# An encoder layer with its FFN in four blocks of 512 tokens, the later blocks' convolution and output projection placed inside the FFN

## The chip, the cores and the metric

The kernel runs on one core of a Trainium2 chip, as one program. Time is device microseconds. Three runs of the kernel before took 2814.54, 2819.62 and 2824.38 us, so its time is 2819.62 us (median). A further execution was taken by the hardware profiler; all rows below come from it.

The engines: PE is TensorE (matmuls and transposes), PEld its weight loads, DVE VectorE, ACT ScalarE, POOL GpSimd, SP the queue that issues every DMA of this kernel.

## The reference

One layer over 2048 prompt tokens of a new stream and 32 tokens of a running stream, all in float32:

```python
xn = rmsnorm(x, g_mix)
q, k, v, u, gate = split(xn @ w_in)                 # 1024 -> 2560
q, k = head_rmsnorm(q, g_q), head_rmsnorm(k, g_k)   # 8 heads of 64
z = q @ k.T * 64 ** -0.5                            # s < t only
sp = softplus(z)
a = exp(log_sigmoid(z) - (reverse_cumsum(sp) - sp)) # stick-breaking weights
o = a @ v
c = causal_dwconv(u * sigmoid(gate), w_dw, 31 taps) # 512 channels
c = silu(layernorm(c))
h = x + concat([o, c]) @ w_out                      # 1024 -> 1024
up = causal_dwconv(rmsnorm(h, g_ffn) @ w_up, 3 taps)# 1024 -> 5632
a, g = split(up)
y = h + (silu(g) * a) @ w_down                      # 2816 -> 1024
```

The running stream's 32 tokens see 1024 cached keys and values and carried convolution states; y, the new keys and values and the new states are returned.

## The kernel before

Every float32 product is three TensorE products. An operand is split into a high part in the rounded format F32R and a rest (`split`, L523: ACT copies the high part, DVE subtracts to get the rest); then high x high, high x rest and rest x high are added up in one PSUM bank. This holds for weights too: each w_in, w_out, w_up and w_down tile is loaded raw and split on chip.

Stages, in program order:

1. Input projection (L780 to L811). Granules of 256 columns of w_in, in two halves of 1024 tokens. u and gate become rows of `cb`, four SBUF tiles with one channel a partition and all tokens along the row (L636). q, k and v are normalised and go to DRAM.
2. Depthwise convolution (`conv`, L537), called once for each half of the tokens: for each of 4 channel tiles, 31 DVE instructions over 1024 or 1086 columns, each a multiply-add with one tap's weight from `wdw`.
3. Attention (`unit`, L861): for each head and each 256 queries, scores, sigmoid (ACT), a running product over the keys (a DVE scan in `survive`, L829), transposes on PE, a split, and the product with the values. The first units' tiles in SBUF take the place of the input projection's weights and tokens.
4. Output projection (`out_chunk`, L1021) in seven chunks of 256 tokens and a last one of 288. w_out is split once and stays in SBUF. The last chunk computes transposed, and the norm of the FFN's first segment is placed inside it (L1096).
5. FFN (L1166) in three segments of 768, 640 and 672 tokens (`SEGS`). For each of 22 column tiles f: `up` loads and splits two w_up tiles (512 KB each), makes 2 x 24 x 2 matmuls into two banks, applies the 3 taps on DVE, the gate, and loads and splits a w_down tile. After each second f, `down` adds two f's products to y. w_up and w_down are loaded and split in each of the three segments: 132 and 66 loads.

The order of instructions is not the program order. `Plan.run` (L231) is a list scheduler: it goes through the recorded steps with a price for each instruction and a latency between engines, and each engine takes the ready step of lowest rank, which is its place in the program. The convolution has ranks behind the whole attention (L1011), so DVE takes it only where nothing else is ready. Which SBUF place a tile takes is written out by hand (`SLOTS`, L46); a tile whose place is still being read has to wait. PSUM has 8 banks, and a rule in `run` keeps one of them for the oldest group that has none.

All DMAs are issued by SP in one order, each with its waits, so a DMA whose wait is late holds up those behind it.

## Time and profile before

| | |
|---|---|
| runs | 2814.54, 2819.62, 2824.38 us |
| profiled execution | 2816.1 us; span from first to last instruction 2814.2 us |
| busy share of the span | PE 96%, PEld 90%, DVE 71%, ACT 39%, POOL 18% |
| mean granted TensorE clock | 0.992 |
| HBM | 217.08 MB read, 64.11 MB written |
| DMA | mean 102 GB/s; 33.3% of the 16 engines' time |

A busy share says that an instruction was in the engine, and matmuls overlap, so a PE at 96% need not issue matmuls as fast as it could. The stages have different limits, so the page's mean is taken apart by stretches: input projection to 580 us, attention from 580 to 1098 us, output projection to 1307 us, FFN to 2810 us.

### The profile page before, as it was taken

The page shows a single profiled execution, that of the slowest core. Times are in us where ns is not written, and L with a number is a line of the kernel's source. Part 1 is how long each engine was busy: PE and PEld are TensorE (multiplying, and loading weights), DVE is VectorE, ACT ScalarE, POOL GpSimd, SP SyncE. Part 2 cuts the span into 40 slices and gives each one's busy share as a digit, 9 for nine tenths or more (in the row PEclk, how much of TensorE's full clock was granted, in tenths as well). Part 3 has the DMA queues.
Part 4 walks back from the last instruction along what each step waited for, and adds up shares of the span by engine and source line. Part 5 has one row for each costly group of instructions (what it writes and reads, how often), then busy time and mean ns, then how long its engine had stood idle before and what let it go on. Part 6 is the DMA issues. An engine that isn't in the chain of part 4 may idle for free.

```text
span 2814.2 us, 43546 instructions
## 1 busy us (share of the span) xinstructions
PE 2690.4 (96%) x17345; PEld 2527.0 (90%) x17345; DVE 2003.1 (71%) x2311; ACT 1103.1 (39%) x2179; POOL 494.3 (18%) x724
## 2 busy tenths in 40 slices
PE   8999999988888888999999999999999999999999
PEld 8999999977777877889999999999999999999998
DVE  6988888899989998345565656666666665656566
ACT  5267235566666675114222222322232233322222
POOL 1155035523223231011000000000000001101100
PEclk9999999999999999999999999999999999999999
DMA  4255224644333335555222222242222233222221
GB/s 161 64 177 175 76 82 152 192 130 116 85 93 85 93 99 159 182 159 170 68 60 68 60 63 72 89 159 71 75 83 75 73 99 103 80 73 64 83 61 70
DMA packets 299907, 288.29 MB, mean 102 GB/s; under 512 B 21591, under 2 KB 260077, under 8 KB 298679
## 3 DMA queue, kind: packets, MB, share of 16 engines
q1 hardware_dynamic: 299703, 285.50, 33.3%
q8 instruction: 136, 2.23, 0.3%
q14 instruction: 68, 0.56, 0.1%
HBM read 217.08 MB, written 64.11 MB: 100 GB/s over the span
## 4 chain that ended last, share of the span: by engine, by line
PE 73%; DVE 10%; issue 6%; POOL 6%; ACT 3%; DMA 2%; SPq 0%; POOLq 0%; DVEq 0%; ACTq 0%
PE bank L380 70%; DVE arena L409 6%; POOL few L409 3%; DVE arena_r L409 3%; PE bank L387 3%; POOL arena L409 3%; ACT arena L394 2%; ACT arena_r L394 1%; DMA arena<-in_cache_sb_v_dram 1%; SPq L434 0%; DMA arena<-arena 0%; DVE few L409 0%; DMA oT_d<-arena 0%; DMA arena<-in_w_ffn_dw_dram 0%; DMA qT_d<-arena_r 0%
## 5 line engine op out<-in xcount | busy, mean ns | idle before, releaser
L380 PE MATMUL bank<-arena_r 128*128 128x256 f32 (+8 forms) x15360 | 2494.5, 322 | 32.4 <-DVE arena_r L409 31.0
L380 PEld LDWEIGHTS bank<-arena_r 128*128 128x128 f32 x15360 | 2320.6, 190 | 157.1 <-DVE arena_r L409 43.3
L409 DVE TENSOR_TENSOR arena_r<-arena,arena_r 128x1024 fp32r<-128x1024 f32 (+5 forms) x398 | 421.7, 1068 | 466.2 <-ACT arena_r L394 462.8
L394 ACT ACTIVATE arena_r<-arena 128x1024 fp32r<-128x1024 f32 (+5 forms) x398 | 368.7, 935 | 911.1 <-PE bank L380 509.8
L394 ACT ACTIVATE arena<-bank 128x384 f32<-128x384 f32 (+15 forms) x770 | 327.6, 473 | 278.2 <-PE bank L380 244.4
L409 DVE TENSOR_TENSOR arena<-bank,arena 128x512 f32<-128x512 f32 (+2 forms) x458 | 281.8, 631 | 189.5 <-PE bank L380 189.2
L409 DVE TENSOR_TENSOR_SCAN arena<-arena 128x1024 f32<-128x1024 f32 (+11 forms) x200 | 330.4, 1680 | 15.1 <-ACT arena L394 7.8
L409 DVE SCALAR_TENSOR_TENSOR arena<-arena,wdw 128x1024 f32<-128x1024 f32 (+1 forms) x240 | 320.6, 1367 | 1.6
L387 PE MATMUL bank<-ident,arena 128*128 128x128 f32 (+4 forms) x1645 | 224.0, 279 | 67.2 <-DVE arena L409 50.6
L387 PEld LDWEIGHTS bank<-ident,arena 128*128 128x128 f32 (+4 forms) x1645 | 185.5, 142 | 100.0 <-DVE arena L409 57.0
L409 POOL COPY halo<-arena 128x2 f32<-128x2 f32 x176 | 80.4, 472 | 1061.8 <-ACT arena L394 1049.8
L394 ACT ACTIVATE arena_r<-bank 128x512 fp32r<-128x512 f32 (+4 forms) x422 | 218.2, 570 | 110.5 <-PE bank L387 98.2
L409 DVE SCALAR_TENSOR_TENSOR arena<-arena,wfd 128x768 f32<-128x768 f32 (+2 forms) x264 | 248.1, 940 | 10.2
L409 DVE TENSOR_TENSOR arena_r<-bank,arena_r 128x512 fp32r<-128x512 f32 (+2 forms) x334 | 194.2, 634 | 18.2 <-ACT arena_r L394 18.0
L409 POOL TENSOR_SCALAR_AFFINE_SELECT arena<-arena 128x128 f32<-128x128 f32 (+1 forms) x130 | 132.8, 1032 | 338.5 <-ACT arena L394 338.1
L394 ACT ACTIVATE arena<-arena 128x1024 bf16<-128x1024 f32 (+4 forms) x100 | 88.2, 882 | 254.3 <-DVE arena L409 237.1
L409 POOL TENSOR_SCALAR few<-few 128x1 f32<-128x1 f32 (+3 forms) x87 | 62.1, 713 | 493.1 <-DVE few L409 405.3
L409 POOL TENSOR_TENSOR few<-few,nhalf 128x1 f32<-128x1 f32 (+3 forms) x87 | 112.0, 1290 | 6.6
L409 DVE TENSOR_TENSOR arena<-arena 128x768 f32<-128x768 f32 (+4 forms) x78 | 68.7, 881 | 46.7 <-ACT arena L394 33.2
L394 ACT ACTIVATE arena<-bank,few 128x64 f32<-128x64 f32 (+1 forms) x272 | 68.6, 325 | 77.9 <-POOL few L409 77.9
L409 DVE TENSOR_SCALAR arena<-arena,wfd,bfd 128x768 f32<-128x768 f32 (+2 forms) x132 | 84.0, 637 | 6.0 <-ACT arena L394 6.0
L409 POOL COPY arena<-halo 128x2 f32<-128x2 f32 x132 | 24.5, 185 | 294.1 <-DVE arena L409 281.7
(43 smaller groups left out, 377.8 us busy)
## 6 DMA issues: line engine op xcount, KB each, us to landing
arena<-in_w_up_dram SPq DMA_DIRECT2D x132, 512.0 KB
arena<-in_w_down_dram SPq DMA_DIRECT2D x66, 512.0 KB
arena<-in_x_prompt_dram SPq DMA_DIRECT2D x32, 512.0 KB
arena_r<-qT_d SPq DMA_DIRECT2D x64, 256.0 KB
arena<-h_d SPq DMA_DIRECT2D x32, 512.0 KB
arena<-in_w_in_dram SPq DMA_DIRECT2D x24, 512.0 KB
arena<-in_w_in_dram SPq DMA_DIRECT2D x32, 256.0 KB
out_dram<-arena SPq DMA_DIRECT2D x32, 256.0 KB
```

Source lines behind the costliest of these rows:

```text
L380: lambda: nc.tensor.matmul(plan.real(out), lhsT, rhs, start=start, stop=stop),
L387: "pe", in_.shape[0] * (0.4167 if in_.dtype == F32R else 0.8333) + 2.5, lambda: nc.tensor.transpose(plan.real(out), in_, idt), [out], [in_ ...
L394: "act", ns, lambda: nc.scalar.activation(out, plan.real(in_), func, **kw), aps(out, kw.get("accum_out")), reads
L409: self.tag, self.price(name, n / (2 if fast else 1), pointers), lambda: fn(out, *map(plan.real, args), **kw), [out], aps(*args, *kw.values())
```

## The change

- The FFN runs in four blocks (`feed`) of 512 tokens, the last of 544 with the running stream's 32. A w_up tile then needs 24 matmuls of 512 columns into one bank, in the last block 48 of 272.
- Block 0 loads raw weights and splits them, in half tiles, and stores the split pairs in DRAM (`wu_d`, `wd_d`: 44 and 22 tiles of 1 MB). Blocks 1 to 3 load the pairs straight into the place that the matmuls read: 1 MB for each w_up and each w_down tile, through two places (`wu`) and three (`wd`).
- u x sigmoid(gate) goes to DRAM (`c_d`); `conv` works on blocks of 512 tokens and loads them from there. Blocks 0 and 1 are convolved behind the input projection as before, block 2 inside the FFN of block 1, block 3 inside that of block 2.
- The output projection (`project`) is cut into the part of the heads and that of the convolution, with h kept in DRAM between them, and into blocks: block 0 before the FFN, block b + 1 inside the FFN of block b. w_out is loaded raw and split for each use (`out_weights`), in the place `wu` that the FFN's weights use, eight pairs of tiles for a block and eight more for the running stream.
- `weave` and `tick` place these pieces: after each `up` part and each `down` tile half the side work is brought up to a given share.
- The planner's prices for matmuls and scans are new, and a new rule (`fits`) says when a group may take a bank ahead of older ones. Constants of the FFN are loaded at the start; several SBUF places are new.

```diff
-SEGS = ((0, 768, 0), (768, 640, 0), (1408, 640, 32))
+BLK = 512
+NBLK = T // BLK
 GRP = 2
...
+        def fits(k):
+            if place[k] == oldest:
+                return True
...
+            if place[k] - oldest > AHEAD:
+                return False
...
-            max(n * 0.4167, width(lhsT) * 0.8333) + 2.5,
+            max(n * 0.4167 + 13, 112),
...
-    vec = Engine("dve", nc.vector, lambda name, n, pointers: n / 0.96 + 68 + 61 * pointers)
+    def vec_price(name, n, pointers):
+        return n * 2.1 + 50 if name == "tensor_tensor_scan" else n / 0.96 + 68 + 61 * pointers
+    vec = Engine("dve", nc.vector, vec_price)
...
+    CB = 30 + T + 30 + TS
+    c_d = dram.tile([SB, CB], F32, name="c_d")[:]
+    wu_d = dram.tile([2 * FT, P, 2048], F32R, name="wu_d")[:]
+    wd_d = dram.tile([FT, P, 2048], F32R, name="wd_d")[:]
...
+    def conv(b):
...
+            pieces = [(b * BLK, BLK)] + ([(T + 30, TS)] if b == NBLK - 1 else [])
+            for t0, m in pieces:
+                src = slot("csrc", (544,))[:, : m + 30]
+                need = ["c0"] + [("c", x) for x in {max(b - 1, 0), b}]
+                dma(src, c_d[c * P : (c + 1) * P, t0 : t0 + m + 30], gets=need)
+                acc = slot("cacc", (m,))
+                for k in (30, *range(30)):
+                    w = wdw[:, k * CT + c : k * CT + c + 1]
+                    if k == 30:
+                        vec.tensor_scalar(acc, src[:, k : k + m], w, cvec[:, c : c + 1], ALU.mult, ALU.add)
+                    else:
+                        vec.scalar_tensor_tensor(acc, src[:, k : k + m], w, acc, ALU.mult, ALU.add)
+                    yield
+                o = t0 if t0 < T else T
+                dma(yT_d[c * P : (c + 1) * P, o : o + m], acc, puts=[("y", b if t0 < T else NBLK)])
...
+        key = [("c", grp[0] // 2)]
+        dma(c_d[ct * P : (ct + 1) * P, o : o + m], sig[:, :m], puts=key)
...
+    def out_weights(i):
+        nh, k = i // 4, i % 4 * 2
+        w = slot("wu", (2, 2, 512), F32R)
+        for j in range(2):
+            raw = slot("raw", (512,))
+            dma(raw, w_out[(k + j) * P : (k + j + 1) * P, nh * 512 : (nh + 1) * 512])
+            split(w[:, 0, j], w[:, 1, j], raw)
+        return w
...
+    def project(b, part, begin):
+        groups = [list(range(4 * b, 4 * b + 4))] + ([[16]] if b == NBLK - 1 else [])
+        for tl in groups:
+            w = sum(tokens(ti)[1] for ti in tl)
+            hi, lo = slot("cat", (CT, w), F32R), slot("cat", (CT, w), F32R)
+            for i in range(0, len(tl), 2):
+                some = tl[i : i + 2]
+                rs = slice(tokens(some[0])[0].start, tokens(some[-1])[0].stop)
+                cs = slice(i * P, i * P + rs.stop - rs.start)
+                fill = conv_out if part else heads_out
+                yield from fill(some, rs, rs.start // BLK, hi[:, :, cs], lo[:, :, cs])
+            for nh in range(2):
+                pss = [bank() for _ in tl]
+                for kk in range(2):
+                    wo = out_weights(4 * nh + 2 * part + kk)
+                    for i, ti in enumerate(tl):
+                        rows = tokens(ti)[1]
+                        for j in range(2):
+                            k = 2 * kk + j
+                            for n, (x, y) in enumerate(((hi, 0), (hi, 1), (lo, 0))):
+                                mm(
+                                    pss[i][:rows],
+                                    x[:, k, i * P : i * P + rows],
+                                    wo[:, y, j],
+                                    start=(k == 0 and n == 0),
+                                    stop=(k == CT - 1 and n == 2),
+                                )
+                    yield
                 cs = slice(nh * 512, (nh + 1) * 512)
-                ps = bank()
-                if joined:
-                    for c in range(4):
-                        tr(ps[:rows, c * P : (c + 1) * P], tt[:, 4 * nh + c, i * P : i * P + rows], ident)
-                else:
-                    mm3(
-                        ps,
-                        lambda k: ch_t[:, k, i * P : (i + 1) * P],
-                        lambda k: cl_t[:, k, i * P : (i + 1) * P],
-                        lambda k: woh[k][nh],
-                        lambda k: wol[k][nh],
-                        KT,
-                    )
-                vec.tensor_tensor(xt[:, cs], ps[:rows], xt[:, cs], ALU.add)
-                if nh == (0 if joined else 1):
-                    dma(h_d[tokens(ti)[0], :], xt, puts=[("h", ti)])
-    gffn = slot("gffn", (D,))
-    dma(gffn, g_ffn.broadcast_to([P, D]))
-    pool.memset(halo, 0.0)
-    wfr = w_ffn_dw.rearrange("k (f p) -> (k f) p", p=P)
-    columns(wfd[:, :66], wfr[:66], 66)
-    columns(wfd[:, 66:], wfr[66:], 66)
-    columns(bfd, b_ffn_dw.rearrange("o (f p) -> (o f) p", p=P), 2 * FT)
-    columns(sfs, state_ffn.rearrange("k (f p) -> (k f) p", p=P), 4 * FT)
+                for i, ti in enumerate(tl):
+                    rs, rows = tokens(ti)
+                    xt = slot("half", (512,))[:rows]
+                    if begin:
+                        dma(xt, x_prompt[rs, cs] if ti < 16 else x_sample[:, cs])
+                    else:
+                        dma(xt, h_d[rs, cs], gets=[("h1", ti, nh)])
+                    vec.tensor_tensor(xt, pss[i][:rows], xt, ALU.add)
+                    dma(h_d[rs, cs], xt, puts=[("h1", ti, nh) if begin else ("h", ti)])
+                yield
+    def n_project(b, part):
...
+            act(x[:rows], x[:rows], AF.Copy, scale=r[:rows])
...
+        total = 2 * FT + 4 * FT
+        done = [0]
+        def tick():
+            done[0] += 1
+            upto(done[0] / total)
...
-                raw = slot("raw4", (KT, P))
-                dma(raw, w_up_v[:, :, fi * P : (fi + 1) * P])
                 wu = slot("wu", (2, KT, P), F32R)
-                split(wu[:, 0], wu[:, 1], raw)
-                ub = slot("ub", (2 + w,))
+                if b == 0:
+                    for j in range(2):
+                        raw = slot("raw", (4, P))
+                        dma(raw, w_up_v[:, 4 * j : 4 * j + 4, fi * P : (fi + 1) * P])
+                        split(wu[:, 0, 4 * j : 4 * j + 4], wu[:, 1, 4 * j : 4 * j + 4], raw)
+                    dma(wu_d[fi], wu.rearrange("p a k n -> p (a k n)"), puts=[("wu", fi)])
+                else:
+                    dma(wu.rearrange("p a k n -> p (a k n)"), wu_d[fi], gets=[("wu", fi)])
...
+            if f == FT - 1:
+                upto(1.0)
...
-            raw = slot("raw4", (D,))
-            dma(raw, w_down[f * P : (f + 1) * P, :])
             wd = slot("wdx" if f == FT - 1 else "wd", (2, D), F32R)
-            split(wd[:, 0], wd[:, 1], raw)
+            if b == 0:
+                for j in range(2):
+                    cs = slice(j * 512, (j + 1) * 512)
+                    raw = slot("raw", (512,))
+                    dma(raw, w_down[f * P : (f + 1) * P, cs])
+                    split(wd[:, 0, cs], wd[:, 1, cs], raw)
+                dma(wd_d[f], wd.rearrange("p a n -> p (a n)"), puts=[("wd", f)])
+            else:
+                dma(wd.rearrange("p a n -> p (a n)"), wd_d[f], gets=[("wd", f)])
...
+    def weave(*steps):
+        side = [[it, n, a, z, 0] for it, n, a, z in steps]
+        def upto(share):
+            for x in side:
+                it, n, a, z, taken = x
+                while x[4] < n and (x[4] < (share - a) / (z - a) * n or share >= 1.0):
+                    x[4] += 1
+                    next(it, None)
+                if x[4] == n:
+                    for _ in it:
+                        pass
+        return upto
+    n_conv = [4 * 31] * (NBLK - 1) + [8 * 31]
+    phase1()
+    attention()
+    mark = len(plan.steps)
+    for i, x in enumerate(convs):
+        x[4] = mark + i / len(convs)
+    normed = []
+    for part in (1, 0):
+        for _ in project(0, part, part):
+            pass
+    normed.append(norm_block(0))
+    for b in range(NBLK - 1):
+        work = []
+        if b:
+            work.append((conv(b + 1), n_conv[b + 1], 0.0, 0.6))
+        work.append((project(b + 1, 0, True), n_project(b + 1, 0), 0.1, 0.55))
+        work.append((project(b + 1, 1, False), n_project(b + 1, 1), 0.65, 0.97))
+        feed(b, weave(*work))
+    feed(NBLK - 1, lambda share: None)
```

**What moves on DVE where the attention starts.** The names: `wdw` marks a convolution tap, rows of `arena<-arena` with 832 to 1024 columns are the attention's scans, 128x8x64 is a split of q, k or v. Before:

```order
L409 SCALAR_TENSOR_TENSOR arena<-arena,wdw 128x1086
L409 SCALAR_TENSOR_TENSOR arena<-arena 128x960
L409 SCALAR_TENSOR_TENSOR arena<-arena,wdw 128x1086
L409 SCALAR_TENSOR_TENSOR arena<-arena 128x960
L409 SCALAR_TENSOR_TENSOR arena<-arena 128x1024
L409 SCALAR_TENSOR_TENSOR arena<-arena 128x832
L409 SCALAR_TENSOR_TENSOR arena<-arena 128x1024
L409 TENSOR_TENSOR arena_r<-arena,arena_r 128x8x64
```

and now:

```order
L444 TENSOR_TENSOR arena_r<-arena,arena_r 128x8x64 x2
L444 TENSOR_TENSOR arena<-arena,bank_62 128x512
L444 TENSOR_TENSOR arena_r<-arena,arena_r 128x8x64
L444 SCALAR_TENSOR_TENSOR arena<-arena 128x960
L444 SCALAR_TENSOR_TENSOR arena<-arena 128x1024
L444 SCALAR_TENSOR_TENSOR arena<-arena 128x960
L444 SCALAR_TENSOR_TENSOR arena<-arena 128x1024
```

Before, taps of 1086 columns stand up to and between the first scans; now the last tap of blocks 0 and 1 is 44 rows of the order earlier, and no tap follows until the FFN.

**What moves on PE where the FFN starts.** `ident` marks a transpose, 128x288 the last output chunk, 128x384 the first segment's `up`, 128x512 x6 one tile's output projection and x24 one `up` part. Before:

```order
L380 MATMUL bank_63<-arena_r 128x288 x8
L380 MATMUL bank_60<-arena_r 128x288 x24
L380 MATMUL bank_58<-arena_r 128x288 x24
L387 MATMUL bank_61<-ident,arena 128x128 x4
L387 MATMUL bank_64<-ident,arena 128x128 x4
L387 MATMUL bank_59<-ident,arena 32x128 x4
L387 MATMUL bank_62<-ident,arena 128x128 x4
L387 MATMUL bank_65<-ident,arena 128x128 x4
L387 MATMUL bank_63<-ident,arena 32x128 x4
L380 MATMUL bank_60<-arena_r 128x384
L380 MATMUL bank_58<-arena_r 128x384
```

and now:

```order
L415 MATMUL bank_58<-arena_r 128x512 x6
L415 MATMUL bank_61<-arena_r 128x512 x6
L422 MATMUL bank_65<-ident,arena 128x128 x4
L422 MATMUL bank_62<-ident,arena 128x128 x4
L422 MATMUL bank_59<-ident,arena 128x128 x4
L422 MATMUL bank_64<-ident,arena 128x128 x4
L422 MATMUL bank_60<-ident,arena 128x128 x4
L422 MATMUL bank_63<-ident,arena 128x128 x4
L422 MATMUL bank_58<-ident,arena 128x128 x4
L422 MATMUL bank_61<-ident,arena 128x128 x4
L415 MATMUL bank_65<-arena_r 128x512 x24
```

Before, matmuls of the output projection stand between the norm's transposes; now all 32 transposes of block 0's norm stand behind the last matmul of its output projection and ahead of the first `up`, with nothing between.

**What moves on SP in the FFN.** Each row is a DMA; `wu_d` and `wd_d` are 1 MB loads of split weights. Before, in the second segment:

```order
L434 DMA arena<-in_w_up_dram 128x8x128 x2
L434 DMA arena<-in_w_down_dram 128x1024
L434 DMA arena<-in_w_up_dram 128x8x128
L434 DMA arena<-in_w_down_dram 128x1024
L434 DMA arena<-h_d 128x1024 x2
```

and now, in block 1:

```order
L473 DMA arena_r<-wu_d 128x2048 x4
L473 DMA arena_r<-wd_d 128x2048 x2
L473 DMA arena_r<-wu_d 128x2048 x4
L473 DMA yT_d<-arena 128x512
L473 DMA arena<-c_d 128x542
L473 DMA arena_r<-wd_d 128x2048 x2
L473 DMA arena_r<-wu_d 128x2048
L473 DMA arena<-in_w_out_dram 128x512 x2
L473 DMA arena_r<-wu_d 128x2048
L473 DMA arena<-in_w_out_dram 128x512 x2
L473 DMA arena_r<-wu_d 128x2048
L473 DMA yT_d<-arena 128x512
```

Where raw tiles of 512 KB went through a buffer of their own to be split, tiles of 1 MB now go straight to the matmuls' two places, and the side work's loads and stores (`c_d`, `in_w_out`, `yT_d`, `h_d`) stand between them in the same queue.

## Rows read from the trace of the kernel before

**Rows 1.** Page, part 1: busy us (share of the span) xinstructions.
```profile
PE 2690.4 (96%) x17345; PEld 2527.0 (90%) x17345; DVE 2003.1 (71%) x2311; ACT 1103.1 (39%) x2179; POOL 494.3 (18%) x724
```

**Rows 2.** Windows: stretch, its us, each engine's busy us, PEclk, DMA share, GB/s.
```profile
100.00:527.00 427.00, 407.25 (x3343) 399.98 (x3342) 367.09 (x371) 204.55 (x520) 183.02 (x122) 1.00 0.38 124
527.00:580.00 53.00, 45.93 (x317) 43.87 (x317) 47.30 (x44) 28.49 (x73) 17.15 (x18) 0.87 0.87 249
580.00:1098.00 518.00, 439.13 (x3070) 391.20 (x3068) 498.27 (x527) 346.83 (x727) 141.68 (x134) 0.98 0.36 98
1098.00:1307.00 209.00, 206.84 (x1088) 176.87 (x1088) 98.86 (x134) 59.10 (x100) 29.07 (x58) 0.99 0.58 176
1307.00:2810.00 1503.00, 1501.19 (x8808) 1426.70 (x8808) 917.22 (x1147) 424.71 (x681) 113.86 (x362) 1.00 0.26 80
```

**Rows 3.** Waits of PE from 100 to 580 us: us, times, longest.
```profile
PE bank L387 <- DVE arena_r L409: 19.3, 18, 2.3
```

**Rows 4.** Windows of the instructions that read wdw: DVE, ACT, PEclk, DMA, GB/s.
```profile
100.00:527.00 427.00, 262.30 (x199) 0.00 (x0) 1.00 0.38 124
527.00:580.00 53.00, 25.24 (x17) 0.00 (x0) 0.87 0.87 249
```

**Rows 5.** Groups by shape: xcount | busy us, mean ns | idle before.
```profile
L409 DVE SCALAR_TENSOR_TENSOR arena<-arena,wdw 128x1086 f32<-128x1086 f32 x120 | 165.9, 1413 | 0.8
...
L409 DVE SCALAR_TENSOR_TENSOR arena<-arena,wfd 128x640 f32<-128x640 f32 x88 | 77.7, 883 | 4.5
...
L409 DVE TENSOR_TENSOR arena_r<-arena,arena_r 128x1024 fp32r<-128x1024 f32 x260 | 317.2, 1222 | 419.4 <-ACT arena_r L394 416.3 <-PE bank L387 3.0
...
L394 ACT ACTIVATE arena<-arena,few 128x1024 f32<-128x1024 f32 x8 | 9.2, 1154 | 2.5 <-POOL few L409 2.5
```

**Rows 6.** Groups by shape, DVE from 580 to 1100 us.
```profile
L409 DVE TENSOR_TENSOR arena_r<-arena,arena_r 128x512 fp32r<-128x512 f32 x12 | 8.2, 687 | 0.0
```

**Rows 7.** Chain of waits in order of time, output projection: start, us, what.
```profile
1158.23 16.34 PE bank L380 x72
1174.57 0.87 PE bank L387 x8
1175.44 19.97 PE bank L380 x88
```

**Rows 8.** Window inside the first FFN segment.
```profile
1500.00:1600.00 100.00, 100.00 (x533) 94.31 (x533) 58.42 (x70) 25.57 (x36) 4.80 (x16) 1.00 0.21 65
```

**Rows 9.** Timeline: start, us, engine, line, operation; a load and its reader.
```profile
2045.58 0.34 SPq L434 DMA_DIRECT2D arena<-in_w_down_dram  x1
...
2049.06 1.06 ACT L394 ACTIVATE arena_r<-arena 128x1024 fp32r<-128x1024 f32 x1 [4.12 <-DMA arena<-in_w_down_dram]
```

**Rows 10.** Window while a 1 MB load of keys runs.
```profile
662.00:663.00 1.00, 1.00 (x12) 1.00 (x10) 1.00 (x3) 1.00 (x4) 0.00 (x0) 1.00 1.03 401
```

**Rows 11.** Timeline of PE: a wait of PE and the next matmuls.
```profile
1098.36 1.29 PE L387 MATMUL bank<-ident,arena 128*128 128x128 f32 x8 [2.60 <-DMA arena<-yT_d]
```

**Rows 12.** Windows behind that wait.
```profile
1099.00:1102.40 3.40, 3.40 (x12) 2.76 (x10) 2.79 (x5) 0.40 (x1) 1.07 (x3) 0.52 1.05 315
1102.50:1106.00 3.50, 3.50 (x21) 2.97 (x20) 2.75 (x6) 3.22 (x6) 0.38 (x2) 1.00 1.09 359
```

**Rows 13.** Timeline of SP: a store of h and the load that follows it.
```profile
1239.63 0.33 SPq L434 DMA_DIRECT2D h_d<-arena  x1
1242.22 0.80 SPq L434 DMA_DIRECT2D arena<-h_d  x2
```

**Rows 14.** Timeline: the norm of one tile, from the loaded h.
```profile
1296.58 1.06 ACT L394 ACTIVATE arena<-arena 128x1024 bf16<-128x1024 f32 x1 [0.16 <-DMA arena<-h_d]
...
1298.97 1.29 DVE L409 SCALAR_TENSOR_TENSOR arena<-arena,few 128x1024 f32<-128x1024 f32 x1 [0.72 <-POOL few L409]
```

More of the change, by code (lines that the diff above doesn't have):

```diff
@@ L139 @@
 BANK = P * 512
+AHEAD = 40
 class Plan:
@@ L270, in run @@
                     y = max(free[x], soon[x][0][0])
-                if x == "pe" and idle and (shut if len(idle) > 1 else any(k == oldest for _, _, k in shut)):
+                if x == "pe" and idle and pick():
                     z = max(free[x], idle[0][0])
@@ new lines, in norm_block, with out @@
+            xs.append(x)
+        def out(k, ps, cs):
+            g = gff[:, k : k + 1]
+            act(hh[:, k, cs], ps, AF.Copy, scale=g)
+            vec.scalar_tensor_tensor(hl[:, k, cs], ps, g, hh[:, k, cs].bitcast(F32), ALU.mult, ALU.subtract)
+        for k in range(KT):
+            ps = bank()
+            for i in range(4):
+                tr(ps[:, i * P : (i + 1) * P], xs[i][:, k * P : (k + 1) * P], ident)
+            out(k, ps, slice(0, BLK))
+        if last:
+            ps = bank(KT, 512 // KT)[:, :, :TS]
+            for k in range(KT):
+                tr(ps[:, k], xs[4][:TS, k * P : (k + 1) * P], ident[:TS, :TS])
+            for k in range(KT):
+                out(k, ps[:, k], slice(BLK, n))
@@ L1200, in up @@
                             )
-                for c in range(2):
+                for c in range(nc_):
                     m = min(cw, n_p - c * cw)
```

408 lines of the change are left out of this document (188 added, 220 removed).

## The prediction

> **What bounds the kernel now.** I read the page's shares first [rows 1]: PE is busy 96% of the span, DVE 71%. That is a mean over stages with different limits, so I then read windows by stage [rows 2]. The reader is to see three limits in them. In the FFN (1307 to 2810 us) PE is busy 1501.19 of 1503 us, and in the output projection 206.84 of 209: these 1712 us are as long as their matmuls. In the attention (580 to 1098) it is DVE, busy 498.27 of 518 us, that leaves PE idle. In the input projection PE is busy 407.25 of 427 us up to 527, and 45.93 of 53 at a granted clock of 0.87 up to 580; the waits of PE name DVE for 19.3 us there [rows 3]. The convolution takes 262.30 and 25.24 us of DVE in those two stretches [rows 4], and none later. So the change can win where DVE holds PE up, some 47 us at most (27 us of PE idle in the input projection and 20 of DVE idle in the attention), plus what work it takes off; and after 1098 us there is no idle time to win, so that each new wait of PE is lost time.
>
> **Input projection.** Half of the convolution (143 us of DVE) leaves it. The order has its last tap well ahead of the attention, so DVE is free at the end of the stage and not much freer before. Of the 19.3 us of waits I take 12, between 0 and 19. The half clock of 527 to 580, 0.13 of 53 us, is 7 us; I take 3 of it, between 0 and 7. Sum -15 (0 to -26).
>
> **Attention.** The 12 splits of w_out leave it, 8.2 us [rows 6], on the engine that bounds it. New prices for scans may use some of the 20 us that DVE idles; I take 4. Sum -12 (0 to -28).
>
> **PE's own work.** 72 matmuls of 512 columns take 16.34 us in the chain, 227 ns each [rows 7]. In the first segment 533 matmuls fill 100 us, 188 ns each [rows 8]; per f these are 96 of 384 columns and 36 of 512, so one of 384 takes 172.9 ns. By the line through both, 0.42 ns a column, I estimate 320 columns at 145.9, 336 at 152.6, 272 at 125.6, 288 at 132.4 ns. `up` before: 2112 x (172.9 + 145.9 + 152.6) ns = 995.6 us. After: 3 x 1056 x 227 + 2112 x 125.6 = 984.4 us. The `down` matmuls keep their shapes. Output projection before: 672 x 227 + 192 x 132.4 = 178.0 us; after, no chunk is computed transposed: 816 x 227 = 185.2 us. And 24 transposes at 0.87 / 8 = 0.109 us go [rows 7], 2.6 us. Sum -11.2 + 7.2 - 2.6 = -7.
>
> **The start of the FFN.** Before, the first segment's norm lay among the last output chunk's matmuls. Now 32 transposes stand right behind block 0's last output matmul and nothing of another kind between; on their path lie, in a row: the last eviction's add, 0.7 us (as the 128x512 of [rows 6]); h stored and loaded, since the load was issued 2.6 us after the store [rows 13]; the load, up to 3.5 us (issue at 2045.58 to its reader at 2049.06, the same 512 KB) [rows 9]; Square to the instruction behind POOL's rstd, 2.4 us [rows 14]; ACT's scale, 1.15 us [rows 5]; and about 1.3 us of transposes and PSUM copies that PE can't run ahead of. That is 11.6 us. A wait of 2.60 us [rows 11] was followed by 3.4 us at a clock of 0.52 [rows 12], so 1.7 us more: 14 with rounding up. Also `cat`, the operand of block 0's output projection, lies where the attention's last products are read, so PE waits for a copy and a split after them: 3 us. Sum +17 (10 to 22).
>
> **The later block boundaries.** There were two, there are three, and the last pieces of the output projection stand close ahead of each: +4 (0 to 10).
>
> **Weights from memory.** A `wu` place comes free at the end of its part of 24 matmuls, 24 x 227 = 5.45 us, and the other place covers exactly one such part. The trace has no 1 MB load of this kind. From below: 512 KB took 3.5 us from issue to reader [rows 9], and another 0.52 MB at the 401 GB/s of a window in which keys are loaded 1 MB at a time [rows 10] add 1.3: 4.8 us. From above, at 249 GB/s [rows 2], it is 5.6. PE's release and SP's issue come on top, so 5.0 to 6.4 against 5.45. The order of block 1 has runs of four parts and then two f's `down` (10.9 us); the third part of a run is the tight one, and its delay covers the fourth's. With about 1 us each, 11 runs in each of blocks 1 and 2 give 22 us; the ends are 0, and 70 if the queue's side work (`c_d`, `in_w_out`, `yT_d`, `h_d` in the same order, each behind its own waits) makes it 3.2 us a run. Block 0 loads 34.6 MB raw and stores 69.2 MB split; with some 22 MB of other transfers that is 126 MB in about 410 us of PE's work, 307 GB/s where the FFN before moved 80 [rows 2]. I take +8, between 0 and the 95 of the third rival. In the last block a part is 48 x 125.6 ns = 6.0 us: +2 (0 to 5). Sum +32.
>
> The Trainium skill (DMA: Bandwidth & Descriptors, Anatomy of one DMA) fits one DMA, issued from another queue than this kernel's, as some 2.0 us and its bytes at 436 GB/s. An estimate by that page is 4.4 us for 1 MB, under the part's 5.45, and would take nearly all of the 22 us away: it speaks for the first rival. No row of this kernel shows a 1 MB load timed from issue to reader.
>
> **What I cost at nothing.** In the FFN DVE was busy 917 of 1503 us. Splits of weights fall from 198 x 1.222 us [rows 5] to 132 halves x 0.69 [rows 6], -150 us; the taps of blocks 2 and 3 come in, 248 at about 0.75 us, an estimate for 512 columns from the 883 ns of 640 [rows 5], and 124 of 32 columns that I put at a quarter of it, +209; 80 half splits of w_out +55. That is about two thirds of the time, and the cover is DVE's idle time between evictions with 8 banks. If taps got ahead of evictions, each would hold a bank 0.75 us longer; the range holds that. The loads of constants that move to the start meet a DMA share of 0.38 [rows 2].
>
> **Sum.** -15 - 12 - 7 + 17 + 4 + 32 = +19 us. The profiled execution took 2816.1 us (span 2814.2), 3.5 below the median of the runs, within their spread; I add to it: 2835 us, slower by 0.5%. What can be told from no change here is about 0.3%, so 2811 to 2828 is "the same".
>
> **Rivals.** First, faster: the reloads stay hidden (5 us instead of 32) and DVE's relief comes near its bounds (-22 and -20). Then -22 - 20 - 7 + 17 + 4 + 5 = -23: 2793 us. For it: the 4.8 us of a load at 401 GB/s. Against it: PE's waits in the input projection were 19.3 us in all, and half of the taps stay in that stage. Second, no change: the reloads cost about 15 us instead of 32, and the sum is +2: 2818 us. For it: the small half-microsecond steps on which it turns. Third, slower still: block 0's traffic becomes the bound. At the 249 GB/s that the queues sustained at a share of 0.87 between 527 and 580 us [rows 2], 126 MB need 506 us where PE's work needs 410, so 96 instead of 8 us there: 2923 us. It decides from 307 GB/s downward. Against it stand 359 GB/s at a share of 1.09 [rows 12] and the 401 GB/s [rows 10], both over a few microseconds only.
>
> The Trainium skill (DMA: Bandwidth & Descriptors, Specifications) gives about 358 GB/s as one core's limit to HBM. An estimate by it is 126 MB in 352 us, under the 410, which speaks against the third rival; but the stretch of [rows 12] ran at 359 GB/s and the stretch of [rows 10] over it, so in this trace that figure is not a ceiling over short stretches.
>
> **Chances.** The forecast 0.37: its own range is 2828 to 2875. The first rival 0.35, the second 0.18, the third 0.10. The forecast and the first rival differ by one term, a load of about 5 us against a cover of 5.45, and I give the forecast the edge because delays of a queue only add. The range, 2775 to 2890, takes in the first rival with the relief at its full bounds (-54 for both, sum -35, 2781), and leaves out most of the third. Faster 0.35; same 0.18; slower 0.37 + 0.10 = 0.47.
>
> **What would show it.** In the waits of PE in blocks 1 and 2: waits for the load of `wu_d`, about 22 of them near 1 us; none would be the first rival. In the timeline of PE ahead of the first 24 matmuls of an `up` part: a gap near 12 us with the transposes in it, and half clock behind it. In the windows of 527 to 580: PE nearly full, and clock above 0.95. The attention about 12 us shorter, and DVE still its bound. In block 0's windows: about 300 GB/s with PE over 97% busy; PE well below that with the DMA share near 1 would be the third rival. What would make the forecast wrong on the other side is a wait that no row here prices: evictions behind taps, or side DMAs whose late waits hold up the reloads by more than 3 us.

## The result and the profile after

The changed kernel takes 2930.34 us (median of 4 runs, 2927.47 to 2931.09), the kernel before 2820.43 us over its runs: 1.039 times as long, 95% interval 1.037 to 1.0409. The forecast was 2835, its range ended at 2890. It went the way that was forecast, and seven times as far: +110 us instead of +15 against the median.

The windows of the profiled execution after (span 2929.0 us), with the columns of [rows 2]; the stretches are the attention, what lies between it and the first `up`, and the four FFN blocks:

```profile
555.00:1091.10 536.10, 464.76 (x3142) 425.35 (x3141) 506.83 (x531) 346.52 (x742) 153.65 (x145) 0.92 0.34 92
1091.10:1202.50 111.40, 59.68 (x250) 47.84 (x251) 37.74 (x54) 32.45 (x49) 4.45 (x12) 0.74 0.62 203
1202.50:1641.00 438.50, 421.75 (x1888) 348.39 (x1886) 302.98 (x468) 162.46 (x270) 30.57 (x109) 0.99 0.88 300
1641.00:2074.50 433.50, 414.08 (x1840) 340.71 (x1840) 296.43 (x452) 84.10 (x136) 37.33 (x104) 0.99 0.61 216
2074.50:2510.00 435.50, 420.36 (x1857) 340.43 (x1858) 313.25 (x569) 89.68 (x151) 36.80 (x103) 0.99 0.58 209
2510.00:2929.00 419.00, 402.81 (x2932) 388.20 (x2931) 199.63 (x320) 70.95 (x201) 31.41 (x173) 1.00 0.45 165
```

Before, PE idled 4 us from 1098 us to the end of the FFN [rows 2]. After, it idles 51.7 us in the second stretch alone (111.40 - 59.68), with the clock at 0.74 over that stretch, and 67.5 us in the four blocks. The attention ends 7.2 us earlier (its successor's first transpose starts at 1091.13 instead of 1098.36 [rows 11]). So the loss is all behind the attention. Waits of PE from 1080 us on (us, times, longest):

```profile
PE bank L415 <- DMA arena_r<-wu_d: 50.3, 22, 14.9
PE bank L422 <- ACT arena L429: 29.2, 5, 16.9
PE bank L415 <- ACT arena_r L429: 26.1, 5, 17.7
PE bank L415 <- DVE arena_r L444: 3.7, 5, 2.0
```

The waits that name ACT lie ahead of the first `up`, all but 6.1 us. PE's timeline there (start, us, what, xcount, in brackets the idle time and its releaser):

```profile
1091.13 1.24 PE L422 MATMUL bank<-ident,arena 128*128 128x128 f32 x8 [2.62 <-DMA arena<-yT_d]
...
1102.42 23.07 PE L415 MATMUL bank<-arena_r 128*128 128x512 f32 x94 [0.53 <-DVE arena_r L444]
1143.23 23.81 PE L415 MATMUL bank<-arena_r 128*128 128x512 f32 x96 [17.73 <-ACT arena_r L429]
1183.94 0.48 PE L422 MATMUL bank<-ident,arena 128*128 128x128 f32 x1 [16.90 <-ACT arena L429]
1192.81 0.47 PE L422 MATMUL bank<-ident,arena 128*128 128x128 f32 x1 [8.39 <-ACT arena L429]
```

Two gaps stand there: one between the convolution's and the heads' part of block 0's output projection (17.73 us), and one for the norm (16.90 and 8.39). The chain of waits in this window says what each consists of (start, us, what):

```profile
1115.37 0.32 SPq L473
...
1118.90 8.08 DMA arena<-oT_d
...
1129.25 3.86 DMA h_d<-arena
...
1135.13 5.60 DMA arena<-oT_d
...
1163.41 5.62 DMA arena<-in_w_down_dram
1169.06 0.64 ACT arena_r L429
1169.72 0.70 DVE arena_r L444
1170.50 7.41 DMA arena<-in_w_up_dram
1177.93 11.38 DMA arena<-h_d
```

In the first gap the loads of the heads (`oT_d`) come in two rounds with a store of `h_d` between: the half tiles of the residual (`half`) are the same SBUF words as the tiles that the heads are loaded into (`tmp`; both start at word 4096 in `SLOTS`), so the second round waits until the first part's h is stored. In the second, an h load takes 11.38 us where 512 KB took 3.48 [rows 9]: eight of them (four for the norm, four for y), three 1 MB stores of split weights and the next weights are under way together. Here SP's queue at the start of block 1, where PE waits 14.86 us for `wu_d`, and PE's rows there and at the start of block 2:

```profile
1611.14 1.01 SPq L473 DMA_DIRECT2D arena_r<-wd_d  x2
1612.55 0.34 SPq L473 DMA_DIRECT2D out_dram<-arena  x1
1612.98 2.21 SPq L473 DMA_DIRECT2D arena<-h_d  x2
1615.31 13.15 SPq L473 DMA_DIRECT2D arena<-oT_d  x8
1628.95 0.33 SPq L473 DMA_DIRECT2D arena<-h_d  x1
1630.13 0.33 SPq L473 DMA_DIRECT2D arena_r<-wu_d  x1
```

```profile
1615.05 11.14 PE L415 MATMUL bank<-arena_r 128*128 128x512 f32 x48
1641.05 45.59 PE L415 MATMUL bank<-arena_r 128*128 128x512 f32 x192 [14.86 <-DMA arena_r<-wu_d]
...
2074.58 83.92 PE L415 MATMUL bank<-arena_r 128*128 128x512 f32 x360 [11.38 <-DMA arena_r<-wu_d]
```

The side work's eight loads of heads (`oT_d`) for the next block hold SP for 13 us, and the reload of a place that was free at 1620.5 us (1615.05 and 24 matmuls of 227 ns) is issued at 1630.13. SP itself was waiting for earlier transfers to land: its waits from 1612 to 1648 us name DMAs for some 19 us, these two most:

```profile
SPq L473 <- DMA arena<-oT_d: 6.2, 8, 1.0
SPq L473 <- DMA arena<-h_d: 4.9, 4, 1.7
```

From 1611 to 1645 us the DMA share is 1.04 at 316 GB/s: a burst of y stores, h, heads, x and weights, all at the moment when a block begins.

```profile
1611.00:1645.00 34.00, 19.14 (x94) 15.93 (x93) 16.43 (x22) 9.20 (x14) 1.25 (x5) 0.80 1.04 316
```

### The profile page after: what moved, and what is told of

Read it like the earlier page. It is cut to its first block, busy times and chain, and to the rows that moved or that the text cites. A ratio compares the mean times of both kernels' runs of the same rounds, so it can differ in the third digit from the quotient of the medians.

```text
span 2929.0 us, 42909 instructions
## 1 busy us (share of the span) xinstructions
PE 2711.2 (93%) x16218; PEld 2411.1 (82%) x16218; DVE 2006.3 (68%) x2879; ACT 1048.4 (36%) x2196; POOL 444.0 (15%) x809
## 4 chain that ended last, share of the span: by engine, by line
PE 66%; DVE 14%; DMA 10%; ACT 3%; issue 2%; POOL 2%; SPq 1%; DVEq 0%; ACTq 0%; POOLq 0%
PE bank L415 63%; DVE arena L444 10%; DMA arena_r<-wu_d 5%; DVE arena_r L444 4%; PE bank L422 3%; ACT arena L429 2%; ACT arena_r L429 2%; DMA arena<-oT_d 1%; POOL few L444 1%; SPq L473 1%; POOL arena L444 1%; DMA arena<-arena 1%; DMA arena<-h_d 1%; DMA wu_d<-arena_r 1%; DMA arena<-in_x_prompt_dram 0%
## 5 line engine op out<-in xcount | busy, mean ns | idle before, releaser
L415 PE MATMUL bank<-arena_r 128*128 128x512 f32 (+7 forms) x14256 | 2522.5, 337 | 114.4 <-DMA arena_r<-wu_d 50.3
L415 PEld LDWEIGHTS bank<-arena_r 128*128 128x128 f32 (+1 forms) x14256 | 2196.9, 191 | 385.7 <-DVE arena_r L444 36.0
L429 ACT ACTIVATE arena<-bank 128x512 f32<-128x512 f32 (+12 forms) x715 | 324.7, 502 | 977.8 <-PE bank L415 900.1
L444 DVE TENSOR_TENSOR arena_r<-arena,arena_r 128x512 fp32r<-128x512 f32 (+2 forms) x420 | 317.7, 767 | 167.8 <-ACT arena_r L429 164.4
L444 DVE TENSOR_TENSOR arena<-bank,arena 128x512 f32<-128x512 f32 (+4 forms) x488 | 308.3, 638 | 179.8 <-PE bank L415 169.3
L429 ACT ACTIVATE arena_r<-arena 128x512 fp32r<-128x512 f32 (+2 forms) x420 | 287.2, 692 | 397.6 <-PE bank L415 155.6
L444 DVE SCALAR_TENSOR_TENSOR arena<-arena,wdw 128x512 f32<-128x512 f32 (+1 forms) x600 | 400.2, 667 | 11.9
L444 DVE TENSOR_TENSOR_SCAN arena<-arena 128x896 f32<-128x896 f32 (+10 forms) x200 | 331.4, 1692 | 2.7 <-ACT arena L429 2.5
L444 DVE SCALAR_TENSOR_TENSOR arena<-arena,wfd 128x512 f32<-128x512 f32 (+1 forms) x352 | 266.5, 757 | 10.7 <-POOL arena L444 0.5
L429 ACT ACTIVATE arena_r<-bank 128x512 fp32r<-128x512 f32 (+3 forms) x388 | 204.5, 574 | 138.3 <-PE bank L422 126.0
L444 DVE TENSOR_TENSOR arena_r<-bank,arena_r 128x512 fp32r<-128x512 f32 (+2 forms) x300 | 176.0, 630 | 15.6 <-ACT arena_r L429 15.2
```

The costliest lines, as they stand in the source:

```text
L415: lambda: nc.tensor.matmul(plan.real(out), lhsT, rhs, start=start, stop=stop),
L429: "act", ns, lambda: nc.scalar.activation(out, plan.real(in_), func, **kw), aps(out, kw.get("accum_out")), reads
L444: self.tag, self.price(name, n / (2 if fast else 1), pointers), lambda: fn(out, *map(plan.real, args), **kw), [out], aps(*args, *kw.values())
```

## The experiments

Times are medians; the kernel before ran beside each. Where no other base is named, an edit is made in the changed kernel. Kernel 3 is the kernel of experiment 3, and so on; kernels 7 and 8 are the first ones under their numbers. `...` in a diff marks what is left out.

**1. Weights split again in every block.**

```diff
-                if b == 0:
+                if True:
                     for j in range(2):
                         raw = slot("raw", (4, P))
...
-                    dma(wu_d[fi], wu.rearrange("p a k n -> p (a k n)"), puts=[("wu", fi)])
-                else:
-                    dma(wu.rearrange("p a k n -> p (a k n)"), wu_d[fi], gets=[("wu", fi)])
...
```

The same is done to w_down.

> Every block loads raw weights and splits them, as block 0 does; nothing is stored in DRAM or reloaded. Theory of block starts (the loss is in serial chains and in bursts of the one DMA queue where a block starts: some 61 us of idle and half clock ahead of the first up, 26 us of waits at the starts of blocks 1 and 2; the rest are waits of 1 to 3 us): the short waits and a part of the burst go, 2870 to 2885 us, with 45 us or more of PE idle left between the attention's end and the first up. Rival, the reloads: they alone are the loss, so it comes near the time before, 2820 to 2835. Rival, DVE: with 198 more pairs of splits at 1.4 us DVE is busy some 280 us more and evictions come late: 2930 or more.

2900.26 us, ratio 1.029 (1.0274 to 1.0305): 30 us gained, outside all three ranges. No wait for `wu_d` is left, but the FFN has some 36 us of others, most behind DVE, where the changed kernel has 12:

```profile
PE bank L415 <- DVE arena_r L444: 19.9, 14, 4.8
PE bank L422 <- DVE arena L444: 10.1, 1, 10.1
PE bank L415 <- ACT arena_r L429: 6.3, 4, 2.1
```

The gaps ahead of the first `up` stay: 17.3, 10.7 and 7.5 us. So the reloads are not the whole loss, and splitting again, beside the convolution, has its price on DVE.

**2. No reloads at all.** The two `else` branches with the loads in blocks 1 to 3 are taken out, so their matmuls read what stands in the places.

> Leaves out the loads of split weights in blocks 1 to 3: their matmuls use what stands in the places. Theory of block starts: PE's 50 us of waits for these loads go, and some 8 us of half clock behind them, so 2865 to 2880; the 52 us of idle ahead of the first up stay. Rival, the reloads: 2820 to 2835. Rival, the stores of block 0: no change within 10 us, 2920 to 2930.

2856.5 us in one run, 74 us less, more than I expected: PE's idle time in the four blocks falls from 67.5 to 6.5 us, and the start keeps its gaps (17.5, 17.2 and 8.1 us). That splits the loss in two: about 74 us hang on the reloads, and 38 above the time before are left, with the start in them.

**3. A place of its own for block 0's half tiles.**

```diff
+    "half0": spots(0, 512, 8),
...
-                    xt = slot("half", (512,))[:rows]
+                    xt = slot("half" if b else "half0", (512,))[:rows]
```

> Only the half tiles of block 0's output projection get a place of their own, so that the loads of the heads no longer wait for the residual's tiles to be stored. Theory of block starts: the wait of 17.7 us for the heads' split falls to about 3 and some half clock goes with it, -15 to -20: 2910 to 2915. Rival, the reloads: no change within 5 us, 2925 to 2935.

2912.56 us, ratio 1.0333 (1.0318 to 1.0349): -18. The wait of 17.7 us is gone from the trace; the norm's remain (15.6, 2.7, 4.8 and 2.7, 25.7 in sum).

**4. The side work's loads held back.** They wait for the load (in block 0, the store) of the third column tile's weights.

```diff
-                    gets=[("o", blk)],
+                    gets=[("o", blk)] + ([("late", min(blk, 3))] if blk else []),
...
-                        dma(xt, x_prompt[rs, cs] if ti < 16 else x_sample[:, cs])
+                        dma(xt, x_prompt[rs, cs] if ti < 16 else x_sample[:, cs], gets=[("late", b)] if b else [])
...
```

> The side work's loads of heads and x (16 of 256 KB a block) wait for the load of the third column tile's weights of the block they are placed in. Theory of block starts: the waits of 14.9 and 11.4 us at the starts of blocks 1 and 2 fall to 2 to 5 us each: -15 to -22, so 2908 to 2915. Rival, the reloads: such a wait is the 1 MB load's own, no change within 5 us, 2925 to 2935.

2917.24 us (2909.30 to 2928.52), ratio 1.034 (1.0321 to 1.036). The time misses its range by 2 us, and the trace is of the slowest execution, 2928.52. In it the waits at the starts of blocks 1 and 2 fall to 3.75 and 2.3 us, as expected, with one of 4.6 us 23 us later in block 2, while the sum of the waits for `wu_d` only falls from 50.3 to 37.1: more of the short ones. The burst was real; the short cover is a second cost.

**5. A third place for w_up's split tiles.**

```diff
-    "wu": spots(16384, 2048, 2),
-    "wd": spots(20480, 2048, 3),
-    "wdx": [26624],
+    "wu": spots(16384, 2048, 3),
+    "wd": spots(22528, 2048, 3),
+    "wdx": [22528],
```

In this kernel and in the first combination below the last column tile's w_down overwrites one that is still to be read; instructions and bytes are the same.

> The split w_up tiles get a third place (the last w_down tile shares one of the three of the others). Without the reloads at all the time was 2856, so all waits for them cost some 74 us. Theory of two costs (bursts at block starts, and a cover of one part that is a little too short for a load): the waits of 0.5 to 3 us inside blocks 1 to 3, 24 us in sum plus the gaps below, go; those of 14.9 and 11.4 us at the starts stay: -20 to -30, 2900 to 2910. Rival, the queue alone: in it a reload is late because transfers are before it, and a third place changes little: 2920 to 2930.

2871.21 us, ratio 1.0186 (1.017 to 1.0201): -59, twice what I expected. All short waits for `wu_d` are gone, and of those at block starts 7.9 and 4.6 us are left, the only two for it:

```profile
PE bank L415 <- DMA arena_r<-wu_d: 12.5, 2, 7.9
```

A load's cover grows from one part (5.45 us) to two, which also takes up half of the burst's delay. Of the single edits that keep every load this is the largest.

**6. The old prices of matmuls and scans.**

```diff
-            max(n * 0.4167 + 13, 112),
+            max(n * 0.4167, width(lhsT) * 0.8333) + 2.5,
...
-        return n * 2.1 + 50 if name == "tensor_tensor_scan" else n / 0.96 + 68 + 61 * pointers
+        return n / 0.96 + 68 + 61 * pointers
```

> Only the planner's prices of matmuls and scans are those of before. Theory that the attention's gain was eaten by the new order (DVE waits 29 us there instead of 21, PE's clock 0.92 instead of 0.97): from the first scan to the attention's end it takes 8 us or more less than 537 us, and the time is about 2920. Rival, the prices do not matter there: 537 us again within 3. The FFN's order changes too, for better or worse by 10 us.

2954.64 us, ratio 1.0472 (1.045 to 1.0495): 24 us worse, and both expectations fail: the attention takes 545 us instead of 537, though its first scan starts at 543.5 instead of 553.8 us. It ends 2 us earlier, so the 24 us are lost behind it, where the waits for `wu_d` are 61.8 us instead of 50.3 and the rest was not taken apart. Two prices changed at once, perhaps against each other; kernels 10 and 11 part them.

**7. The start in order, and all edits together.** Edits 3 and 4; the loads of y wait like the side loads; the first column tile's stores wait for the norm's loads.

```diff
-                    dma(wu_d[fi], wu.rearrange("p a k n -> p (a k n)"), puts=[("wu", fi)])
+                    dma(wu_d[fi], wu.rearrange("p a k n -> p (a k n)"), gets=[("norm", 0)] if f == 0 else [], puts=[("wu", fi)] + ([("late", 1)] if fi == 2 else []))
...
-            dma(y[:rows], h_d[rs, :], gets=[("h", tix)])
+                dma(y[:rows], h_d[rs, :], gets=[("h", tix), ("late", b + 1)])
...
```

> Own place for block 0's half tiles, side loads held back as before; the loads of y and the first stores of split weights wait until the loads of the norm are issued or landed. Theory of block starts: the idle of PE between the attention's end and the first up falls from 52 to about 22 us (17 from the half tiles, some 13 from the 4 MB that the norm's loads no longer share the queues with), half clock with it, and the boundaries give 20: 2880 to 2890. Rival, the norm's chain is latency alone: 2895 to 2905.

2888.1 us, ratio 1.0243 (1.0228 to 1.0258): the stretch from the attention's end to the first `up` loses some 32 of its 111 us. The norm's gaps fall to 8.1, 2.7, 3.7 and 0.6 us, 15.0 in sum: the norm's loads had been slowed by the transfers beside them, and what stays is the chain. With edit 5 on top:

> All of the edits together: places and order at the start, side loads late, three places for w_up. If the costs of starts and reloads are separate and all told they are the loss, about 2929 - 35 - 20 - 25 = 2850; with the attention's 7 us of gain that leaves it 30 above the time before, or some 1%. Rival, the costs overlap: 2870 or more.

2833.98 us, ratio 1.0054 (1.0039 to 1.0069), 16 us below the sum that I had made, mostly because the third place gives more than the 25 in it. With w_down's last tile in places that are free (10240, in the last block 14336):

> The combination again, with the last column tile's w_down in a place of its own instead of one that is shared: the same time as before this mending, 2830 to 2840. If the shared place had hidden a wait, 2845 or more.

2838.58 us, ratio 1.0067 (1.0053 to 1.0081).

**8. The start filled.** Kernel 7 in its last form, with the heads' part of block 1's output projection in front of block 0's norm, with places of its own for the heads, the half tiles and `cat`.

```diff
     for part in (1, 0):
         for _ in project(0, part, part):
             pass
+    for _ in project(1, 0, True):
+        pass
     normed.append(norm_block(0))
...
```

> Besides, the heads' part of block 1's output projection (96 matmuls, 22 us) stands between block 0's and its norm instead of inside block 0's FFN. Theory of block starts: the norm's chain of stores, loads and rstd (19 us of PE idle left, half clock behind it) is hidden by that work: -18 to -24, 2810 to 2818, the time before or just under it. Rival, the chain only moves: the added stores and loads stand ahead of the norm's in the queue and the gap stays: 2830 or more.

2816.41 us, ratio 0.999 (0.9981 to 0.9998). The norm's 32 transposes now follow the matmuls with no wait:

```profile
1127.09 43.38 PE L419 MATMUL bank<-arena_r 128*128 128x512 f32 x190 [1.46 <-DVE arena_r L448]
1170.31 3.65 PE L426 MATMUL bank<-ident,arena 128*128 128x128 f32 x32
1173.72 26.56 PE L419 MATMUL bank<-arena_r 128*128 128x512 f32 x116
```

Places, order and cover have taken back the 110 us, and no transfer was left out for it. Then block 0's convolution tiles in places that are free during the attention:

```diff
+    "c0": spots(14856, 1024, 2),
...
-        yt = slot("tmp", (CT, w))
+        t = "tmp" if blk else "c0"
+        yt = slot(t, (CT, w))
...
```

> Besides, the convolution tiles of block 0's output projection get places that are free during the attention, so that their loads and transposes can run before it ends. Theory: PE's 7 us of waits behind the attention's last matmul and some half clock go: 2803 to 2811. Rival, DVE bounds the attention and takes the 6 us of norm work there: no change against the kernel without this edit, within 3 us.

2819.87 us, ratio 1.0001 (0.9992 to 1.001): nothing gained. PE's waits around the attention's end are now 4.15 us for DVE, 4.73 for `yT_d` and 4.33 for DVE, where they were 2.3, 1.6 and 3.0. The time is 3.5 us above the kernel without the edit, half a microsecond outside the rival's range. The rival fits best, but the run does not show that DVE's extra work is the cause.

**9. Does DVE's work set the attention's length?**

```diff
-        for h, p in UNITS:
+        for n, (h, p) in enumerate(UNITS):
+            if 10 <= n < 41:
+                next(c2)
...
```

Here `c2` is the convolution of block 2.

> The kernel of the change with one edit: 31 taps of block 2's convolution (0.74 us each, 23 us of DVE) run inside the attention instead of the FFN. Theory of gaps (the w_out splits of before stood in holes in which DVE waited for ACT and PE, so taking them out only left 29 us of holes instead of 21): the stretch from the first scan to the attention's end grows by 0 to 10 us from 537. Rival, DVE's work itself is the attention's length: it grows by 20 to 25 us.

2953.46 us, ratio 1.0458 (1.0435 to 1.0481). From the first scan to its end the attention takes 557.8 us instead of 537.4: +20.5 for 23 us of taps. The theory of holes falls; DVE's work does count there nearly one for one.

**10 to 12. One price each, and the bank rule,** in the first kernel of 8 (2816 us). The scan price:

```diff
-        return n * 2.1 + 50 if name == "tensor_tensor_scan" else n / 0.96 + 68 + 61 * pointers
+        return n / 0.96 + 68 + 61 * pointers
```

> The last combination (start filled with block 1's heads part, 2816 us), with the planner's price of a scan as before. Theory that the price of scans shapes the attention's holes: the attention's stretch (first scan to its end, 536 us there) changes by 5 us or more, and the time with it: 2806 to 2811, or 2822 to 2830 if the true price is the better one. Rival, no price matters there: 2813 to 2820 and 534 to 538.

The matmul price:

```diff
-            max(n * 0.4167 + 13, 112),
+            max(n * 0.4167, width(lhsT) * 0.8333) + 2.5,
```

> The same, with the planner's price of a matmul as before and that of a scan as changed. With both old the attention took 545 us from a first scan 10 us earlier, and the FFN lost 20 us or so. Theory that the matmul price placed the FFN's work: 2825 to 2840, most of it in the FFN. Rival, it was the scan price: 2813 to 2820 here.

The bank rule:

```diff
-AHEAD = 40
+AHEAD = 4
```

> The same, with the new bank rule held closer to the old: a group may be 4 places ahead of the oldest one without a bank instead of 40. Theory that the new rule lets PE run ahead in the attention and come late to what DVE waits for, so that DVE idles 29 us instead of 21: the stretch falls by 5 us or more from 536, and DVE's idle in it to 24 or less. Rival, the rule has no part in it: 534 to 538 us, or longer as PE is held back more.

Old scan price: 2838.51 us, ratio 1.0078 (1.0063 to 1.0093). Old matmul price: 2792.5 us, ratio 0.9913 (0.9898 to 0.9928), the fastest kernel of all. Both lie outside the ranges of theory and rival. Bank rule: 3165.47 us, ratio 1.1232 (1.121 to 1.1253); it holds PE back everywhere and says nothing on the eight microseconds. The attention's stretch, from the first scan to its end, in windows with the columns of [rows 2] (DVE's is the number with some 530 instructions behind it). The kernel before:

```profile
561.24:1098.36 537.12, 453.13 (x3140) 404.16 (x3138) 515.82 (x543) 358.82 (x752) 146.34 (x139) 0.97 0.37 103
```

The changed kernel:

```profile
553.77:1091.13 537.36, 465.99 (x3147) 426.44 (x3145) 508.06 (x531) 347.35 (x744) 153.65 (x145) 0.92 0.34 93
```

Kernel 8:

```profile
553.62:1089.63 536.01, 465.96 (x3146) 426.05 (x3145) 510.15 (x533) 347.18 (x745) 135.75 (x144) 0.92 0.37 101
```

Kernel 10, with the old scan price:

```profile
553.84:1111.67 557.83, 463.34 (x3145) 415.13 (x3143) 519.52 (x537) 352.88 (x748) 137.31 (x145) 0.95 0.36 98
```

Kernel 11, with the old matmul price:

```profile
541.17:1069.57 528.40, 455.17 (x3142) 415.29 (x3140) 509.53 (x532) 347.51 (x744) 130.49 (x144) 0.95 0.37 102
```

DVE's idle time in it is 21.3, 29.3, 25.9, 38.3 and 18.9 us. The new scan price is worth 22 us there. The new matmul price costs 8 us there and lets the first scan start 12 us later. The recalibration was two edits of opposite sign here, and the one that is nearer to the measured 227 ns is the one that costs. Why the planner's order for it is the worse one stays open: the runs show the two orders, not which step of them decides.

## Why the prediction was wrong

**Input projection, -15:** the first scan starts 7.5 us earlier. Right in kind, half the size. Between 527 and 580 us the clock was 0.97 where it had been 0.87 [rows 2]. With the old matmul price the first scan is 20 us earlier: the relief was there, and the new order gave 12 us of it back.

**Attention, -12:** 0. DVE's work did fall (508.06 us instead of 515.82), but DVE idles 8 us more. Its waits for ACT's half of the splits rise from 5.0 to 16.7 us and those for PE from none to 6.4, while those for ACT's other results fall from 8.8 to 3.0. Before:

```profile
DVE arena_r L409 <- ACT arena_r L394: 5.0, 9, 0.9
```

and after:

```profile
DVE arena_r L444 <- ACT arena_r L429: 16.7, 30, 1.8
DVE arena L444 <- PE bank L415: 6.4, 3, 2.4
```

I had allowed the new prices a gain of 4 us and took them as one edit; it is two. Together they do gain 8 us in this stretch (545.3 us with both old, kernel 6), so the term that I had at nothing is the rest of the change, whose new order made the stretch 8 us longer at the old prices although the splits had left. Which part of the change did that stays open. Kernel 9 speaks against the splits having been free, and kernel 11 shows that the matmul price gives 8 us of the scan price's gain back: without it DVE's wait for PE is 0.5 us.

**PE's own work, -7:** holds as far as rows show it. 1048 matmuls of 512 columns run in 238.14 us in block 0, 227 ns each, as in [rows 7]:

```profile
1228.52 238.14 PE L415 MATMUL bank<-arena_r 128*128 128x512 f32 x1048 [1.80 <-ACT arena_r L429]
```

**The start of the FFN, +17:** this is the step that failed worst. The stretch of 111.40 us has 192 matmuls and 56 transposes, 49.7 us of work by the prices of the prediction: 62 us lost, of which 51.7 are PE's idle time and the rest half clock. I priced one chain, and each transfer in it by its time when it runs alone. There were two: I took the gap between the two parts for a copy and a split (3 us) and missed that `half` and `tmp` are the same words, which put a store, a load and 17.7 us between them (kernel 3). And the norm's loads shared the queues with some 6 MB that nobody needed yet, 3 of stores, 2 for y and the next weights (28.5 us of gaps in the changed kernel, 25.7 in kernel 3, 15.0 in kernel 7). What kernel 7 has left is 3 us over the 12 that the prediction had for the chain alone.

**The later boundaries, +4:** 26.2 us, the waits of 14.86 and 11.38 us at the starts of blocks 1 and 2. The prediction named side DMAs ahead of the reloads as what could go wrong, and priced them inside the blocks only; they come in a burst where a block begins (kernel 4).

**Weights from memory, +32:** the mechanism held: 20 waits besides those two, 24 us in sum, where 22 + 2 were forecast. That the sums agree is luck: blocks 1 and 2 have 11 such waits with 14.9 us, where 22 with 22 us were forecast, and the last block, where a part covers more, has 9 with 9.2 us for the 2 forecast:

```profile
PE bank L415 <- DMA arena_r<-wu_d: 9.2, 9, 2.1
```

A 1 MB reload that runs alone is there 4.8 us after its issue (the one issued at 1664.91, by the trace's semaphore events), at the lower bound of the prediction. One beside a `wd_d` load takes longer; here SP's issues in block 1, two loads each (the second of a pair is issued as its duration ends):

```profile
1675.11 1.89 SPq L473 DMA_DIRECT2D arena_r<-wd_d  x2
1681.23 5.76 SPq L473 DMA_DIRECT2D arena_r<-wu_d  x2
```

The reload issued at 1681.23 ends PE's wait at 1687.63, 6.4 us later, about 1 us too late for the third part of a run, as PE's timeline says:

```profile
1687.63 2.55 PE L415 MATMUL bank<-arena_r 128*128 128x512 f32 x10 [0.99 <-DMA arena_r<-wu_d]
```

Block 0's traffic did not bind, as forecast: PE was full in the middle of block 0 at 294 GB/s.

```profile
1300.00:1600.00 300.00, 300.00 (x1341) 248.65 (x1340) 210.77 (x333) 105.86 (x179) 20.33 (x72) 1.00 0.85 294
```

The 4.4 us that the prediction estimated by the Trainium skill (DMA: Bandwidth & Descriptors, Anatomy of one DMA) are 0.4 us short of the lone reload and 2 us short of this one; the measured times decide.

What I missed is that the reloads' cost and the boundary's are one thing: with two places a lone reload has 0.6 us of slack (5.45 - 4.8), so each larger disturbance of the queue reaches PE. A third place removed 59 us, not 24.

**Hidden work.** DVE was busy 1112 us in the four blocks, 64%, against two thirds forecast, and PE's waits for DVE and ACT there are 12 us. That cover held, but for these 12.

The terms: -7.5 + 0 - 7 + 62 + 26 + 41 (67.5 - 26.2) = +114.5, where the -7 is the forecast's. The two profiled spans differ by 114.8 us (2929.0 - 2814.2), the medians by 110. PE's 4 us of idle time before and the half clock inside the blocks after are not in this sum.

**The rivals.** The third (bandwidth of block 0) gave a time near the measured one, 2923, and for a wrong reason: 300 GB/s were sustained over the 438 us of block 0. The first assumed hidden reloads; with three places they are hidden, and kernel 8 then lands near where the second rival put it, at 2816.

## What to carry to other kernels

Before a round trip through memory is priced, look up which SBUF words its tiles share with what runs just before: a shared place turns two parallel chains into one serial one. Price a transfer by its time in the company that it will have, above all where a loop's next block starts and every stage prefetches at once. And a load whose cover equals its latency is not hidden: count slack in whole steps of the loop, and buy one more place before anything else. A planner's recalibration is as many edits as it has prices; each wants its own run, since a truer price can give a worse order.

## What the runs showed of the hardware

One queue sustained 300 GB/s over the 438 us of block 0, loads and stores mixed, at a DMA share of 0.88, and 294 over the 300 us shown above, in which PE was full; the 249 GB/s of [rows 2] was no limit. Here a load's time depended on its company more than on its size: 512 KB of w_down took 3.48 us in the FFN before [rows 9], 512 KB of h 11.38 us in the burst ahead of the first `up`; a 1 MB reload took 4.8 us alone, and the one issued at 1630.13 ended PE's wait at 1641.05, 10.9 us later. PE's gaps at the start cost about a fifth on top of themselves (62 us lost for 51.7 of gaps): the clock stood at 0.74 over the stretch with 51.7 us of gaps, and at 0.92 in kernel 8, where the gaps were filled:

```profile
1091.00:1180.00 89.00, 82.66 (x367) 67.63 (x366) 52.45 (x77) 40.98 (x63) 4.64 (x13) 0.92 0.80 266
```
